# A margin between an operand's planned time and TensorE's step, and durations taken from the trace, in the planner of an encoder block

## The chip, the cores and the metric

The kernel runs on one core of a Trainium2 chip. The metric is the device time of one launch in microseconds (us). Before the change three runs gave 1043.59, 1044.0 and 1044.48 us; the median is 1044.0. The execution that was profiled took 1043.74 us; its span, which the profile's times count from, is 1042.0 us.

## The reference

One layer of an encoder over 528 rows (16 meta tokens and 512 tokens) of 1024 channels, in float32. Two attention branches read the same normalized input and one projection matrix; gates merge them; a mixture of 16 experts follows, in which each expert picks 66 of the 528 rows.

```python
u = rms_norm(h, g_mix)
qa, ka, va, qb, kb, vb, ga, gb = split(u @ w_in)
# branch a: 8 differential heads, d = 64, values of 128
p = softmax(q k^T / 8 - slope * distance)      # two maps per head
oa = rms_norm((p[0] - lam * p[1]) @ va, g_subln) * (1 - lam_init)
# branch b: 8 query heads over 2 key/value heads, d = 128
qh = axial_rope(rms_norm(qb, g_qnorm)); kh = axial_rope(rms_norm(kb, g_knorm))
ob = softmax(qh kh^T / sqrt(128)) @ vb
h = h + (sigmoid(ga) * (oa @ w_branch_a) + sigmoid(gb) * (ob @ w_branch_b)) @ w_out
h = h + expert_choice_ffn(rms_norm(h, g_ffn), w_router, w_gate, w_up, w_down)
return rms_norm(h, g_final)[meta rows dropped]
```

## The kernel before

Every float32 operand is split into a high and a low part (`u_h`, `u_l`; `wh`, `wl`), and each product is three matmuls: high by high, low by high, high by low. A projection of 128 channels runs over 8 chunks of the depth and over two halves of the 528 columns (256 and 272), so a half is 24 rows `pz<-u_h,wh`, `pz<-u_l,wh`, `pz<-u_h,wl` on TensorE. In the names, `pz`, `psc` and `ptr` are the PSUM tiles, two buffers of each: `pz` for projections, values and spread norms, `psc` for scores, `ptr` for transposes.

The work goes in this order. The input is normalized and transposed. Then come 8 differential heads: a head's scores (`psc<-kbuf,qh`), its exponentials (`sn`), their transposes (`ptr<-ident,sn`), the value product (`pz<-wth,vh`, ...), and its norm over channels (`pz<-sqh,sel`; the sums turned by `ptr<-ident,rows`; a root by GpSimd's pow on `cols`; `pz<-ident,cols`). Between a head's steps stand the projections of the next head. For a head, copies between partitions on SyncE's queue lay out its queries and keys (`kbuf<-qh`, `kbuf<-ql`, `qh<-ql`, `kbuf<-kbuf`, `kbh<-kbuf`). Then come 8 GQA heads: scores (`psc<-kbh,qh`), exponentials into `pb` by ScalarE, a scaling of `pb` by the reciprocal sums on VectorE, a small copy (`widen`), transposes (`ptr<-ident,pb`), and the value product, mixed with the projections of the next head's queries and with the products of branch a's output (`pz<-oah,wh`, ...). Then the gates, the output product, the router and the experts.

The program text doesn't set the order within an engine. Each instruction is recorded by a planner, the class `Pace`, which keeps a planned time for each engine (`t`) and for each operand (`ready`), with durations estimated by `Op.price` and a fixed latency of 220 ns (`LAT`) between engines. Instructions of TensorE and DMA starts are put out as the program calls them (`Pace.call`); those of ScalarE, VectorE and GpSimd wait in a list and are put out by `Pace.pump` when their planned start comes within 200 ns of TensorE's planned time (`AHEAD`), by a priority. All instructions pass through one line, L199 in the profile, so a line tells nothing and rows are read by tile names.

TensorE's order comes from `mix`. It has the head's own steps (`main`), the other products as filling (`fill`, in pieces of 6 rows) and small tasks (transposes, value products, norms), which `tick` steps whenever `ok` lets them. `ok` is where a step is held back: all its operands must be planned ready (`pace.when`) by TensorE's planned time, and the PSUM buffers it needs must be free. While a step is held, filling goes ahead of it. On the chip each engine takes its own instructions in the order so fixed and waits where an operand isn't there.

```python
def ok(need, own=None):
    now = pace.now()
    if any(pace.when(a) > now for a in need.tiles):
        return False
...
Task(weigh(i, wt, combine, f"av{NH + h - 1}", ...), Need([ls, p]), ["sn"])
```

`spare_engine` chooses GpSimd or VectorE for some products (`wl`) by GpSimd's planned time, so it reads the same estimates.

Of the kernel before, what the change touches and what calls it, by code (L numbers as in the profile page):

```python
# [15 lines left out]
OP = mybir.AluOpType  # L16
# [69 lines left out]
class Op:  # L86
    def __init__(self, eng, op, fn, args, kw, prio):
        self.eng, self.op, self.fn, self.args, self.kw, self.prio = eng, op, fn, args, kw, prio
        aps = [getattr(a, "ap", a) if isinstance(a, bass.IndirectOffsetOnAxis) else a
               for a in list(args) + list(kw.values())]  # L90
        aps = [a for a in aps if isinstance(a, bass.AP)]
        outs = [kw["out"] if "out" in kw else args[0]]
        if kw.get("accum_out") is not None:
            outs.append(kw["accum_out"])
        self.outs = outs
        self.writes = set().union(*map(keys, outs))
        self.names = self.writes.union(*map(keys, aps))
        self.tiles = {a.name for a in aps + outs}
        self.cost = self.price(aps)

    def price(self, aps):
        n = 1
        for d in self.outs[0].shape[1:]:
            n *= d
        if "dma" in self.op:
            return (CAP * D if "indirect" in self.op else n * self.outs[0].shape[0]) * 4 / 360.0
        if self.op == "transpose":
            return aps[1].shape[0] / 1.2
        if self.eng == "tensor":
            n = 1  # L110
            for d in self.kw["rhs"].shape[1:]:
                n *= d
            return max(107.0, n / 2.4 + 2.5)
        if self.eng == "scalar":
            return 65.0 + n / 1.2 + (90.0 if len(self.outs) > 1 else 0.0)
        if self.eng == "gpsimd":
            return 60.0 + n * 2.27
        if self.op in ("tensor_scalar", "tensor_copy", "memset"):
            return 60.0 + n * 0.65
        return 60.0 + max([n] + [a.free_size() for a in aps if callable(a.free_size)]) / 0.96  # L120
# [5 lines left out]
class Pace:  # L126
# [5 lines left out]
    def __init__(self):  # L132
        self.t = {}
        self.ready, self.by, self.used, self.floor, self.slots = {}, {}, {}, {}, {}
        self.pending, self.busy = [], set()
        self.prio = 1

    def now(self):
# [36 lines left out]
    def start(self, op):  # L175
        start = self.t.get(op.eng, 0.0)
        dma = "dma" in op.op
        for a in op.tiles:
            start = max(start, self.floor.get(a, 0.0) + self.LAT)
        for a in op.names:  # L180
            lat = self.LAT if dma or self.by.get(a) != op.eng else 0.0 if op.eng == "tensor" else 130.0
            start = max(start, self.ready.get(a, 0.0) + lat)
        return start

    def emit(self, op):
        start, eng = self.start(op), op.eng
        if "dma" in op.op:
            issue = 500.0 if eng != "gpsimd" else 1000.0 if "indirect" in op.op else 1300.0
            self.t[eng] = max(self.t.get(eng, 0.0), start if eng == "gpsimd" else 0.0) + issue
            lead = issue + 650.0 if eng == "gpsimd" else 1300.0  # L190
            self.t["dma"] = max(self.t.get("dma", 0.0), start + lead) + op.cost
            end, eng = self.t["dma"] + 850.0, "dma"
        else:
            end = self.t[eng] = start + op.cost
        for a in op.tiles:
            self.used[a] = max(self.used.get(a, 0.0), end)
        for a in op.writes:
            self.ready[a], self.by[a] = end, eng
        op.fn(*op.args, **op.kw)  # L199
# [93 lines left out]
def block_kernel(ctx: ExitStack, tc: tile.TileContext, x, meta_tokens, g_mix, w_cols,  # L293
# [3 lines left out]
    pace = Pace()  # L297
# [45 lines left out]

    tasks = []

    def ok(need, own=None):
        now = pace.now()
        if any(pace.when(a) > now for a in need.tiles):
            return False
        if any(n in t.holds for n in need.names for t in tasks if t is not own):  # L350
            return False
        if need.sn and sum("sn" in t.holds for t in tasks) >= need.sn:
            return False
        return all(n == 0 or pace.free(("psum", tag), 2, n) <= now for tag, n in need.res)
# [13 lines left out]
    def tick():  # L368
        for t in list(tasks):
            if t in tasks and ok(t.need, t):  # L370
                t.step()
# [48 lines left out]
    def mm(out, lhsT, rhs, start, stop, **kw):  # L420
        nc.tensor.matmul(out, lhsT=lhsT, rhs=rhs, start=start, stop=stop, **kw)
# [523 lines left out]
    def mix(main, fill, nfill, steps=5):  # L945
        done, i, fneed = 0, 0, None
        need = next(main)
        while main is not None or fill is not None:
            tick()
            if main is not None and (need is None or (fill is None or done >= i * nfill / steps) and ok(need)):  # L950
                i += need is not None
                try:
                    need = next(main)
                except StopIteration:
                    main = None
            elif fill is not None and (fneed is None or ok(fneed) or not wait()):
                try:
                    fneed = next(fill)
                    done += fneed is None
                except StopIteration:  # L960
                    fill = None
            elif fill is not None:
                pass
            elif not wait():
                if tasks:
                    force()
                else:
                    need = None
# [486 lines left out]
    for r in range(rounds):  # L1455
        rsl = slice(8 * r, 8 * r + 8)
        now, nxt = ping[(r + 1) % 2] if r else pf[:2 * NE, :HL], ping[r % 2]
# [279 lines left out]
    a, b = slice(0, 768), slice(768, D)  # L1737
# [51 lines left out]
```

## Time and profile before

| | before |
|---|---|
| median of three runs | 1044.0 us |
| profiled execution, span | 1043.74 us, 1042.0 us |
| TensorE busy in the span | 958.8 us (92%) |
| TensorE busy, 28 to 571 us | 512.63 of 543.00 us |
| VectorE, ScalarE, GpSimd busy, 28 to 571 us | 355.02, 307.57, 188.75 us |

The profile is one execution. PE is TensorE, DVE VectorE, ACT ScalarE, POOL GpSimd, SP SyncE. A row of the timeline has a start, a length and an operation; in brackets stand the idle time of its engine just before it and what ended that. PEclk is the share of full speed that TensorE's clock was granted. A matmul's length is longer than the distance to the next one, since matmuls overlap; what a row costs is read from the distance of two starts. The stretch from 28 to 571 us holds the two attention branches with their projections, up to the last GQA head.

### The profile page before, as it was taken

What the parts mean: (1) busy time and instruction counts of PE and PEld (TensorE: products, weight loads), DVE (VectorE), ACT (ScalarE), POOL (GpSimd) and SP (SyncE); (2) the same over time, 40 slices, a digit from 0 to 9 for tenths busy, and PEclk for the clock granted to TensorE, in tenths of its full rate; (3) what the DMA queues carried; (4) which work ended last, traced back from release to release, by engine and by line L of the source; (5) the groups of instructions that cost most, each with busy time, mean ns of one, the idle gap of its engine ahead of it and who ended that gap; (6) DMA issues with size and microseconds to landing.
All of it is one profiled execution on the core that took longest, in us unless ns stands there. A gap on an engine that the chain in (4) does not pass through costs nothing.

```text
span 1042.0 us, 18075 instructions
## 1 busy us (share of the span) xinstructions
PE 958.8 (92%) x6835; PEld 830.5 (80%) x6835; DVE 729.0 (70%) x1390; ACT 629.6 (60%) x1297; POOL 311.3 (30%) x354
## 2 busy tenths in 40 slices
PE   4799999999999999999999999995699999999994
PEld 4799989999988899999999999994356666666563
DVE  6357777767774766665665336557699999999886
ACT  5366656666665545555545533344488888888784
POOL 3233232322443434423332400000324342423141
PEclk9999999999999999999999999998799999999997
DMA  7543544444122122121122464834799999999965
GB/s 253 161 136 94 144 124 121 123 108 125 57 72 72 52 72 71 52 72 52 62 62 63 139 201 165 321 121 165 237 355 372 354 374 353 371 348 364 369 218 182
DMA packets 59617, 186.43 MB, mean 179 GB/s; under 512 B 6766, under 2 KB 6907, under 8 KB 59530
## 3 DMA queue, kind: packets, MB, share of 16 engines
q0 software_dynamic: 26544, 98.37, 27.3%
q1 hardware_dynamic: 32378, 84.74, 26.2%
q10 hardware_dynamic: 608, 2.16, 0.7%
q8 instruction: 54, 0.88, 0.3%
q14 instruction: 33, 0.27, 0.1%
HBM read 164.23 MB, written 10.76 MB: 168 GB/s over the span
## 4 chain that ended last, share of the span: by engine, by line
PE 65%; DVE 15%; ACT 7%; issue 4%; POOL 4%; DMA 3%; SPq 1%; POOLq 0%; ACTq 0%; DVEq 0%
PE pz L199 40%; PE psc L199 21%; PE ptr L199 5%; DVE sn L199 3%; POOL cols L199 3%; ACT sn L199 2%; DVE cols L199 1%; DVE pb L199 1%; SPq L199 1%; DVE wtl L199 1%; DVE ls L199 1%; DVE zb L199 1%; DMA zp<-zb 1%; DMA xin<-in_x_dram 1%; POOL wl L199 1%
## 5 line engine op out<-in xcount | busy, mean ns | idle before, releaser
L199 PE MATMUL pz<-u_h,wh 128*128 128x256 f32 (+1 forms) x832 | 246.2, 296 | 5.9 <-ACT u_h L199 1.8
L199 POOL TENSOR_TENSOR wl<-wraw,wh 128x512 fp32r<-128x512 f32 x106 | 142.1, 1347 | 345.9 <-ACT wh L199 341.0
L199 PE MATMUL pz<-u_l,wh 128*128 128x256 f32 (+1 forms) x832 | 238.1, 286 | 0.5 <-DVE u_l L199 0.5
L199 PE MATMUL pz<-u_h,wl 128*128 128x256 f32 (+1 forms) x832 | 238.0, 286 | 0.6 <-DVE wl L199 0.6
L199 DVE TENSOR_TENSOR el<-raw,eh 128x1024 fp32r<-128x1024 f32 x180 | 212.8, 1224 | 8.1 <-ACT eh L199 7.2
L199 ACT CAST eh<-raw 128x1024 fp32r<-128x1024 f32 x180 | 181.3, 1049 | 20.6 <-PE pz L199 13.5
L199 PEld LDWEIGHTS pz<-u_h,wh 128*128 128x128 f32 x832 | 158.1, 190 | 9.2 <-DVE kbuf L199 2.3
L199 PEld LDWEIGHTS pz<-u_l,wh 128*128 128x128 f32 x832 | 158.3, 190 | 0.7 <-DVE u_l L199 0.7
L199 PEld LDWEIGHTS pz<-u_h,wl 128*128 128x128 f32 x832 | 158.1, 190 | 0.8 <-DVE wl L199 0.8
L199 PE MATMUL psc<-eh,xh 128*66 128x512 f32 (+1 forms) x272 | 104.8, 385 | 2.7 <-ACT hid L199 2.2
L199 ACT CAST wh<-wraw 128x512 fp32r<-128x512 f32 x152 | 90.9, 616 | 23.4 <-PE pz L199 19.5
L199 PE MATMUL psc<-el,xh 128*66 128x512 f32 (+1 forms) x272 | 103.8, 381 | 0.1
L199 PE MATMUL psc<-eh,xl 128*66 128x512 f32 (+1 forms) x272 | 103.7, 381 | 0.0
L199 DVE TENSOR_TENSOR wtl<-ptr,wth 128x512 fp32r<-128x512 f32 (+1 forms) x72 | 46.0, 638 | 59.0 <-ACT wth L199 58.7
L199 PE MATMUL pz<-eh,hhl 128*66 128x512 f32 x224 | 70.7, 396 | 0.7 <-DVE hhl L199 0.6
L199 ACT ACTIVATE sn<-sn,nm 128x528 f32<-128x528 f32 x64 | 47.1, 735 | 35.2 <-DVE nm L199 34.8
L199 POOL DMA_INDIRECT acc<-ys,idxu x15 | 27.5, 1835 | 122.0 <-ACT ys L199 97.1
L199 ACT CAST wth<-ptr 128x512 fp32r<-128x512 f32 (+1 forms) x72 | 39.0, 542 | 40.4 <-PE ptr L199 40.0
L199 PEld LDWEIGHTS psc<-eh,xh 128*66 128x66 f32 x272 | 37.4, 137 | 25.1 <-ACT hid L199 3.2
L199 PEld LDWEIGHTS psc<-el,xh 128*66 128x66 f32 x272 | 37.3, 137 | 23.4 <-DVE el L199 0.5
L199 PEld LDWEIGHTS psc<-eh,xl 128*66 128x66 f32 x272 | 37.4, 137 | 21.8 <-DVE xl L199 0.5
L199 DVE CUSTOM_DVE_ANT_0 sn<-psc,m 128x528 f32<-128x528 f32 x64 | 44.1, 695 | 5.8 <-PE psc L199 5.8
(315 smaller groups left out, 2328.3 us busy)
## 6 DMA issues: line engine op xcount, KB each, us to landing
wraw<-in_w_in_dram SPq DMA_DIRECT2D x76, 512.0 KB, 3.6
raw<-in_w_up_dram POOLq DMA_DIRECT2D x14, 2048.0 KB, 17.3
raw<-in_w_down_dram POOLq DMA_DIRECT2D x14, 2048.0 KB, 20.2
raw<-in_w_gate_dram POOLq DMA_DIRECT2D x13, 2048.0 KB, 18.7
m<-in_c_bias_dram SPq DMA_DIRECT2D x8, 1056.0 KB, 7.0
kbuf<-kbuf SPq DMA_DIRECT2D x32, 132.0 KB, 2.4
raw<-in_w_up_dram SPq DMA_DIRECT2D x2, 2048.0 KB
raw<-in_w_gate_dram SPq DMA_DIRECT2D x2, 2048.0 KB, 10.5
```

The source lines that it names most:

```text
L199: op.fn(*op.args, **op.kw)
```

## The change

`ok` adds a margin, SLACK = 600 ns: an operand must be planned ready that long before TensorE's planned time. The estimates in `Op.price` take other durations: a matmul 0.4375 ns a column plus 6 (at least 109) instead of 1/2.4 plus 2.5 (at least 107), ScalarE 75 ns more for an activation and 30 for a copy, GpSimd 1150 ns for a pow and 30 ns more for the rest. And a VectorE operation with at least two operands, all in SBUF, that would start within GpSimd's latest operation is planned at that operation's end (`port`). No operation is added to the computation; the list of instructions comes out in another order.

```diff
--- before.py
+++ after.py
@@ -97,6 +97,8 @@
         self.names = self.writes.union(*map(keys, aps))
         self.tiles = {a.name for a in aps + outs}
         self.cost = self.price(aps)
+        ins = [a for a in aps if not a.name.startswith(("pz", "psc", "ptr"))]
+        self.port = eng == "vector" and "dma" not in op and len(ins) >= 2 and len(ins) == len(aps)
 
     def price(self, aps):
         n = 1
@@ -110,11 +112,14 @@
             n = 1
             for d in self.kw["rhs"].shape[1:]:
                 n *= d
-            return max(107.0, n / 2.4 + 2.5)
+            return max(109.0, n * 0.4375 + 6.0)
         if self.eng == "scalar":
-            return 65.0 + n / 1.2 + (90.0 if len(self.outs) > 1 else 0.0)
+            scaled = 75.0 if self.op == "activation" else 30.0
+            return 65.0 + scaled + n / 1.2 + (90.0 if len(self.outs) > 1 else 0.0)
         if self.eng == "gpsimd":
-            return 60.0 + n * 2.27
+            if self.kw.get("op") == OP.pow:
+                return 1150.0
+            return 90.0 + n * 2.27
         if self.op in ("tensor_scalar", "tensor_copy", "memset"):
             return 60.0 + n * 0.65
         return 60.0 + max([n] + [a.free_size() for a in aps if callable(a.free_size)]) / 0.96
@@ -133,6 +138,7 @@
         self.t = {}
         self.ready, self.by, self.used, self.floor, self.slots = {}, {}, {}, {}, {}
         self.pending, self.busy = [], set()
+        self.pool = 0.0, 0.0
         self.prio = 1
 
     def now(self):
@@ -180,6 +186,8 @@
         for a in op.names:
             lat = self.LAT if dma or self.by.get(a) != op.eng else 0.0 if op.eng == "tensor" else 130.0
             start = max(start, self.ready.get(a, 0.0) + lat)
+        if op.port and self.pool[0] < start < self.pool[1]:
+            start = self.pool[1]
         return start
 
     def emit(self, op):
@@ -192,6 +200,8 @@
             end, eng = self.t["dma"] + 850.0, "dma"
         else:
             end = self.t[eng] = start + op.cost
+            if eng == "gpsimd":
+                self.pool = start, end
         for a in op.tiles:
             self.used[a] = max(self.used.get(a, 0.0), end)
         for a in op.writes:
@@ -343,9 +353,11 @@
 
     tasks = []
 
+    SLACK = 600.0
+
     def ok(need, own=None):
         now = pace.now()
-        if any(pace.when(a) > now for a in need.tiles):
+        if any(pace.when(a) + SLACK > now for a in need.tiles):
             return False
         if any(n in t.holds for n in need.names for t in tasks if t is not own):
             return False
```

Below, rows of each engine's order before and of the changed kernel; the line is L199 before and L209 in the changed kernel.

SyncE's queue at the start, before: `wraw` are loads of projection weights, `m` of the position bias, the rest are the first head's copies between partitions.

```order
L199 DMA wraw<-in_w_in_dram 128x1024 x3
L199 DMA kbuf<-qh 64x528
L199 DMA kbuf<-ql 64x528
L199 DMA qh<-ql 64x528
L199 DMA kbuf<-kbuf 64x528 x2
L199 DMA kbh_204<-kbuf 64x528 x2
L199 DMA wraw<-in_w_in_dram 128x1024
L199 DMA kbuf<-kbuf 64x528 x2
L199 DMA m_197<-in_c_bias_dram 128x4x528
```

The changed kernel, the same place:

```order
L209 DMA wraw<-in_w_in_dram 128x1024 x2
L209 DMA kbuf<-qh 64x528
L209 DMA kbuf<-ql 64x528
L209 DMA wraw<-in_w_in_dram 128x1024
L209 DMA qh<-ql 64x528
L209 DMA kbuf<-kbuf 64x528 x2
L209 DMA kbh_204<-kbuf 64x528 x2
L209 DMA kbuf<-kbuf 64x528 x2
L209 DMA wraw<-in_w_in_dram 128x1024
L209 DMA m_197<-in_c_bias_dram 128x4x528
```

The first two copies moved ahead of one load of weights, and the last two ahead of another.

TensorE in the GQA head around 414 us, at the second score product of the head; `pz<-oah,wh` and the rows like it are the products of branch a. Before:

```order
L199 MATMUL psc<-kbh_202,qh 128x264
L199 MATMUL psc<-kbl_203,qh 128x264
L199 MATMUL psc<-kbh_202,ql 128x264
L199 MATMUL ptr<-ident,pb 128x128 x4
L199 MATMUL ptr<-ident,pb 48x128
L199 MATMUL pz<-oah,wh 128x272
L199 MATMUL pz<-oal,wh 128x272
L199 MATMUL pz<-oah,wl 128x272
```

The changed kernel, the same head (eight rows of the branch product of 272 columns stand where the mark is):

```order
L209 MATMUL psc<-kbh_202,qh 128x264
L209 MATMUL psc<-kbl_203,qh 128x264
L209 MATMUL psc<-kbh_202,ql 128x264
L209 MATMUL pz<-oah,wh 128x272
L209 MATMUL pz<-oal,wh 128x272
L209 MATMUL pz<-oah,wl 128x272
...
L209 MATMUL pz<-oah,wl 128x272
L209 MATMUL ptr<-ident,pb 128x128 x4
L209 MATMUL ptr<-ident,pb 48x128
```

The transposes of `pb`, which followed the score product directly, now follow 12 rows of the branch product.

VectorE in the next GQA head, from where the norm's sums arrive (`cols_8x<-ptr`) to the scaling of `pb`; `cols<-cols_8x` takes up GpSimd's root. Before:

```order
L199 TENSOR_SCALAR cols_80<-ptr 128x4
L199 TENSOR_SCALAR cols_80<-ptr 16x1
L199 TENSOR_TENSOR ql<-zb,qh 128x528
L199 TENSOR_SCALAR cols<-cols_80 128x5 x2
L199 RECIPROCAL ls<-ls 128x1
L199 TENSOR_SCALAR pb<-pb,ls 128x528
L199 SCALAR_TENSOR_TENSOR m_197<-m_197,pz 128x256
L199 TENSOR_REDUCE nmb<-psc 128x1
```

The changed kernel:

```order
L209 RECIPROCAL ls<-ls 128x1
L209 TENSOR_SCALAR pb<-pb,ls 128x528
L209 TENSOR_SCALAR cols_81<-ptr 128x4
L209 TENSOR_SCALAR cols_81<-ptr 16x1
L209 SCALAR_TENSOR_TENSOR m_197<-m_197,pz 128x256
L209 TENSOR_REDUCE nmb<-psc 128x1
L209 TENSOR_TENSOR wtl<-ptr,wth 128x4x128
L209 SCALAR_TENSOR_TENSOR wm<-ptr,sign,stk 48x128
L209 TENSOR_TENSOR nmb<-nmb,cols 128x1
L209 TENSOR_SCALAR cols<-cols_81 128x5 x2
```

The scaling of `pb` came behind the root's result and now stands ahead of the sums' arrival; the root's result is taken up after it and after a further reduction and a pair of transposes' evictions.

## Rows read from the trace of the kernel before

**Rows 1.** Busy time and share of the span, from the page's first part
```profile
PE 958.8 (92%) x6835; PEld 830.5 (80%) x6835; DVE 729.0 (70%) x1390; ACT 629.6 (60%) x1297; POOL 311.3 (30%) x354
```

**Rows 2.** Windows: length; busy us (instructions) of PE, PEld, DVE, ACT, POOL; clock; DMA; GB/s
```profile
28.00:571.00 543.00, 512.63 (x4153) 499.90 (x4152) 355.02 (x812) 307.57 (x816) 188.75 (x216) 0.99 0.32 90
...
281.00:385.00 104.00, 97.03 (x777) 93.33 (x777) 68.23 (x145) 57.41 (x149) 46.96 (x59) 1.00 0.22 63
```

**Rows 3.** Waits of TensorE in 28 to 571 us: total, times, longest
```profile
PE ptr L199 <- DVE pb L199: 8.2, 7, 1.4
PE pz L199 <- POOL cols L199: 8.0, 8, 1.4
PE psc L199 <- DMA kbuf<-kbuf: 6.2, 1, 6.2
PE pz L199 <- DVE kbuf L199: 1.7, 3, 0.7
```

**Rows 4.** Timeline of TensorE at the start: start, length, operation, [idle before <- releaser]
```profile
40.03 0.28 PE L199 MATMUL pz<-u_h,wh 128*128 128x256 f32 x1
40.15 0.28 PE L199 MATMUL pz<-u_l,wh 128*128 128x256 f32 x1
...
49.12 1.47 PE L199 MATMUL psc<-kbuf,qh 128*128 128x264 f32 x4 [6.25 <-DMA kbuf<-kbuf]
...
51.27 0.41 PE L199 MATMUL pz<-u_h,wh 128*128 128x256 f32 x1
51.48 0.41 PE L199 MATMUL pz<-u_l,wh 128*128 128x256 f32 x1
```

**Rows 5.** Windows around the first score product
```profile
48.00:50.00 2.00, 0.88 (x3) 0.72 (x4) 0.00 (x0) 0.00 (x0) 0.00 (x0) 0.50 1.06 305
...
54.00:56.00 2.00, 2.00 (x17) 2.00 (x17) 1.15 (x3) 0.60 (x2) 0.00 (x0) 0.91 0.00 0
```

**Rows 6.** Timeline of SyncE's queue at the start
```profile
34.25 0.33 SPq L199 DMA_DIRECT2D wraw<-in_w_in_dram  x1
34.63 0.56 SPq L199 DMA_DIRECT2D kbuf<-qh  x1
...
39.67 0.46 SPq L199 DMA_DIRECT2D qh<-ql  x1
...
56.98 0.47 SPq L199 DMA_DIRECT2D kbuf<-qh  x1
...
59.26 0.46 SPq L199 DMA_DIRECT2D qh<-ql  x1
```

**Rows 7.** Timeline of VectorE at the start
```profile
31.77 0.44 DVE L199 TENSOR_TENSOR ql<-pz,qh 128x272 fp32r<-128x272 f32 x1 [1.14 <-ACT qh L199]
32.87 1.30 DVE L199 TENSOR_TENSOR wl<-wraw,wh 128x512 fp32r<-128x512 f32 x1 [0.65 <-ACT wh L199]
```

**Rows 8.** Timeline of several engines in a steady GQA head
```profile
408.00 0.49 PE L199 MATMUL ptr<-ident,rows 128*128 128x128 f32 x3
...
409.04 1.17 POOL L199 TENSOR_TENSOR cols<-cols,halfs 128x5 f32<-128x5 f32 x1 [1.95 <-DVE cols L199]
...
411.27 2.52 POOL L199 TENSOR_TENSOR wl<-wraw,wh 128x512 fp32r<-128x512 f32 x2
...
411.34 1.32 DVE L199 TENSOR_SCALAR cols<-cols 128x5 f32<-128x5 f32 x2 [1.17 <-POOL cols L199]
...
412.76 1.32 DVE L199 TENSOR_SCALAR pb<-pb,ls 128x528 f32<-128x528 f32 x1
...
414.23 0.73 PE L199 MATMUL ptr<-ident,pb 128*128 128x128 f32 x5 [1.42 <-DVE pb L199]
...
416.74 0.50 DVE L199 TENSOR_SCALAR pb<-pb,ls 128x528 f32<-128x528 f32 x1
```

**Rows 9.** Timeline of TensorE in the second and third differential head
```profile
136.29 0.76 PE L199 MATMUL pz<-ident,cols 128*128 128x128 f32 x5 [1.15 <-POOL cols L199]
...
152.65 0.39 PE L199 MATMUL pz<-u_h,wh 128*128 128x272 f32 x1 [0.81 <-ACT oa L199]
```

## The prediction

> **What bounds the kernel now.** I read the page first: TensorE is busy for 958.8 us, 92% of the span [rows 1]. A reorder can therefore only take TensorE's idle time, and only where the order of its rows differs. In the order of the changed kernel TensorE's rows are those of before from about 579 us on, so the second look was at the stretch before that: from 28 to 571 us TensorE is busy for 512.63 of 543.00 us, idle for 30.4 [rows 2]. That is the room, and 104 us of it (281 to 385) hold 7.0 [rows 2]. Third, the waits of that stretch [rows 3]: 8.2 us for pb (the exp'd scores of a GQA head after DVE has scaled them), 8.0 for cols (POOL's root of the norm), 6.2 in one piece for the first head's kbuf copies, and 1.7 for kbuf; the table's last groups (oa, sql, zv and other small ones) 4.5 us. All are waits of TensorE for an operand made by another engine, or for a PSUM slot that such an engine clears. So the reader is to see that TensorE is the bound, with holes, and that each hole names its maker.
>
> **The change part by part.** It adds and removes no instruction of any weight; it moves them. Where the margin asks that an operand be ready 600 ns before TensorE's planned time, the planner puts other rows (projection or branch products) ahead of the step that waits. A row of 256 columns costs 0.12 us at full clock [rows 4], so 6 rows put 0.7 us and 12 rows 1.4 to 1.5 us in front.
>
> *The start.* TensorE waits 6.25 us until 49.12 for the first score product, for DMA kbuf<-kbuf [rows 4]. The granted clock in 48 to 50 us is 0.50, the lower of the two levels (1.2 GHz), after TensorE had stood still, and in 54 to 56 it is 0.91 [rows 5]. 0.09 short of 1 over 2 us is 0.36 us at half, so the low stretch lasts from 49.12 to 54.36, 5.2 us, and half of that, 2.6 us, is lost; the rows show it, 0.21 us apart against 0.12 [rows 4]. Both hang on SyncE's queue. There the first copy, kbuf<-qh, goes out at 34.63, behind a weight load that left at 34.25 [rows 6]. That load waited for its buffer: DVE's wl product began at 32.87 and took 1.30, until 34.17 [rows 7]. But the copy's data were done at 31.77 + 0.44 = 32.21 [rows 7]. In the changed order the two copies stand ahead of that load, so they can go at 32.2, 2.4 us earlier. The next step, qh<-ql, went at 39.67, 5.0 us after the first copy; in the second head it goes 2.3 us after (56.98 to 59.26), with no load on the queue just ahead of them [rows 6]. With 2.3 the step goes at 34.6 in place of 39.67, 5.1 us earlier, and everything behind it too: the score product could start at 44.0. With 5.0 it goes at 37.2 and the product at 46.7. TensorE comes to it at 49.12 - 6.25 = 42.87, plus six projection rows that now stand ahead: 43.6. So the wait is 0.4 us (then no drop of the clock) or 3.1. I take the first, since the second head's rows are the same copies without a load ahead: 6.25 - 0.4 + 2.6 = **8.4 us** off. Bounds: 8.9 (nothing left) and 3.1 (wait of 3.1, clock still falling).
>
> The Trainium skill ("DMA: Bandwidth & Descriptors", section on queues, rings and completion order) says that descriptors on one ring of an SDMA engine are consumed in ring order. The 5.0 against 2.3 us agree with it: the small copy stood behind 512 KB. It also speaks against me, since that load now stands ahead of qh<-ql and the copies after it: by it the product would start up to 2.7 us later (5.0 less 2.3), the term would be 5.7 and the time 1027.0 instead of 1024.3.
>
> *The GQA heads.* Five heads wait 1.41 us or so each at the same step: the rows' transposes at 408.00, POOL's pow 409.04 (1.17 us) and four small POOL operations, DVE's scaled cols at 411.34 (1.32 us), the scaling of pb at 412.76 (1.32 us, beside two POOL products of 2.52 us together from 411.27; 0.50 at 416.74, after them), TensorE at 414.23 after a wait of 1.42 [rows 8]. In the changed order DVE scales pb before it takes POOL's root (cols) in all these heads, so the wait for POOL (1.17 us) and the 1.32 us of cols are off pb's path. In two of them 12 branch rows besides stand between the score product and the transposes of pb, 1.5 us more cover against 1.42 of wait; there a wl product (1.30 us, as at 32.87 [rows 7]) has come ahead of the scaling on DVE. So I count the whole group, **8.2 us** [rows 3]. If pb is late again in half of the seven, it is 4.
>
> A rule that speaks against this term: the Trainium skill ("SBUF — State Buffer", section SBUF: two separate sides) has the port pair that VectorE shares with GpSimd as an exclusive lock for the whole instruction. The two lengths of the scaling, 1.32 and 0.50 us, agree in kind: DVE takes longer while POOL multiplies. The planner's new port test only delays a DVE operation that starts inside POOL's latest operation. What the rule makes of the time is the third rival.
>
> *The waits for cols.* Eight, together 8.0 us [rows 3]: four in the differential heads, all like that of 1.15 us at 136.29 [rows 9], so 4.6, and 3.4 in the turn from one branch to the other. In the changed order the first head has 42 rows in place of 34 between the transposes of rows and the product on cols (-1.1). In the others there are 22 for 34 and 29 for 42, some 1.5 us less cover; but a POOL product (1.26 us, half of the 2.52 [rows 8]) that stood between pow and the small operations now stands ahead of pow. The two cancel, and I count nothing there; of the turn's 3.4 us I count half, since most of its distances grow: **2.8 us**. Bounds: a loss of 4 (five heads that had no such wait get 0.8) and a gain of 6.
>
> *The other waits.* Kbuf's three waits and the small ones (oa, sql, zv and so on) add to 6.2 us [rows 3]; half lie in the turn, where the margin moves rows ahead. I take **2 us**; bounds 0 and 4.
>
> *What the order adds.* The value product of 272 columns now comes 6 rows behind that of 256 in most differential heads (12 before, in some). Six rows are 0.7 us, and the wait for oa was 0.81 us where ACT came to it late [rows 9]. I count **2 us** of new waits over all 16 heads; bounds 0 and 8 (ten such waits). The margin puts no wait on an engine's queue: it is only read while the order is made. The new prices of ACT and POOL alone move operations between DVE and POOL (a wl product goes to DVE in some heads, 1.3 us as at 32.87 [rows 7]); DVE is busy for 355.02 of the 543 us [rows 2], so I give that no price of its own; where it stands ahead of pb it is in the bound of that term.
>
> The sum: -8.4 - 8.2 - 2.8 - 2 + 2 = **-19.4 us**. Against the profiled execution's 1043.74 us (span 1042.0) that is 1024.3; the median of the runs, 1044.0, is 0.3 above it. I predict 1024.5.
>
> **The rivals.**
> 1. *Only the start comes free.* The planner's times are sums of estimates; with higher prices its clock for TensorE moves too, and the margin may be eaten by errors that add up over a head. For it: the scaling of pb took 1.32 us at one place and 0.50 at another [rows 8]. Against: the moves stand at the very place of the wait. Then -8.4, and 1 us of new waits: 1036.3.
> 2. *Slots take the place of operands.* With rows of projections pulled forward, the two PSUM buffers of a kind are asked for sooner after their last use. For it: 0.81 us for oa, a wait for a slot [rows 9]. Against: in the waits of before, pb, cols and the copies make 22.4 of the 28.6 us [rows 3]. At 0.8 us in each of 16 heads it adds 12.8 rather than 2 to the sum: -8.6, 1035.
> 3. *The shared port.* If POOL's product again falls on the scaling of pb in the five heads, 0.82 us each (1.32 less 0.50) stay, 4.1 us: 1028.4.
> 4. *Slower: the filling runs out.* A head has a fixed number of foreign rows to be mixed in. What the margin puts early is missing at the head's end, where the chain from rows to pb (408.00 to 414.23, 6.2 us [rows 8]) or the value product then has nothing beside it. It decides from the point where this uncovered piece is over 1.2 us a head in 16 heads, 19.4 us. At 1.42, the longest wait of this kind now, it is 22.7: 1047. Against it: in the changed order the branch rows still reach each head's end.
> 5. *It does nothing.* The margin would have to leave the order alone; the rows of the changed kernel show that it doesn't, so this has a chance only as gains and losses that cancel.
>
> **How the numbers follow.** The forecast 0.56 (its own range 1019 to 1030); the first rival 0.10 and the second 0.12; the third 0.14; the fourth 0.04; the fifth 0.04. The low end is every term at its better bound: -8.9 - 8.2 - 6 - 4 = -27.1, so 1016.6; the high end takes in rivals 1 to 3 (1036.3). I set 1016.5 to 1036.5. What a measurement of this kernel can tell from no change is about 0.2%, 2 us: faster by more than that 0.92, within it 0.04, slower 0.04.
>
> **What would show it.** In the profile after: the first score product at 43.5 to 45 us with a wait under 1 us, and no slice of PEclk at 0.5 behind it; if the wait is over 3 us, the start's term is wrong. In the table of waits, pb under 2 us in all and no 1.4 us wait repeated in the GQA heads; cols at about 5 us, still in the differential heads; TensorE idle for about 13 to 15 us between 28 us and the end of the last GQA head, which comes near 552. New waits for oa, zv or kbuf over 6 us in all would speak for the second rival; DVE's scaling of pb at 1.3 us again, with pb in the waits, for the third. Any difference after the gates (the order there is unchanged) would contradict the whole reading.

## The result, and the profile after

The changed kernel took 1035.01 us (median of four, 1032.82 to 1037.56), before 1044.24: a ratio of 0.9913, with a 95% interval of 0.9886 to 0.994. That is 9.2 us faster, where 19.5 were forecast: inside the range, but less than half the size. Its profiled execution took 1036.38 us, span 1034.6. One of the six executions of e14, further down, took 1582.62 us at a granted clock of 0.56; it is in that run's median (1037.92) and not in its ratio, and the other five have a median of 1036.55.

By the page's first part TensorE is busy for 960.1 us, 93% of the span. In the stretch that was the room for the change (columns as in [rows 2]):

```profile
28.00:571.00 543.00, 520.98 (x4232) 508.87 (x4232) 335.90 (x815) 308.02 (x823) 191.69 (x217) 1.00 0.33 92
```

22.0 us idle, where there were 30.4 [rows 2]: 8.4 us went. The table of waits in the same stretch (total, times, longest) says which:

```profile
PE ptr L209 <- DVE wtl L209: 5.9, 6, 2.2
PE pz L209 <- POOL cols L209: 3.2, 6, 1.1
PE psc L209 <- DMA kbuf<-kbuf: 2.8, 2, 1.5
PE pz L209 <- DVE kbuf L209: 2.6, 2, 1.3
PE ptr L209 <- ACT sn L209: 2.4, 3, 0.8
PE pz L209 <- DVE zb L209: 1.9, 2, 1.6
PE pz L209 <- DVE oa L209: 1.6, 2, 1.4
```

Pb is gone from it (8.2 us [rows 3]), cols fell from 8.0 to 3.2, the copies from 6.2 to 2.8. But 5.9 us for wtl are new, 2.4 for sn, 1.9 for zb, and kbuf rose from 1.7 to 2.6. Wtl is VectorE's part of emptying a transpose's PSUM tile, so transposes now wait for a buffer where they waited for their operand. (The table takes in waits over 0.15 us. VectorE's oa, 1.6, is new as well; ScalarE's oa, sqb and zv have 1.1 left.)

**The start.** TensorE's two waits (start, length, operation, idle before and its releaser), against one of 6.25 us [rows 4]:

```profile
44.03 0.36 PE L209 MATMUL psc<-kbuf,qh 128*128 128x264 f32 x1 [1.52 <-DMA kbuf<-kbuf]
45.66 1.03 PE L209 MATMUL psc<-kbuf,qh 128*128 128x264 f32 x3 [1.27 <-DMA kbuf<-kbuf]
```

SyncE's queue, against [rows 6]:

```profile
30.68 0.56 SPq L209 DMA_DIRECT2D kbuf<-qh  x1
...
33.16 0.34 SPq L209 DMA_DIRECT2D wraw<-in_w_in_dram  x1
33.55 0.46 SPq L209 DMA_DIRECT2D qh<-ql  x1
...
35.40 1.20 SPq L209 DMA_DIRECT2D kbh<-kbuf  x2
39.73 1.28 SPq L209 DMA_DIRECT2D kbuf<-kbuf  x2
41.11 0.57 SPq L209 DMA_DIRECT2D wraw<-in_w_in_dram  x1
41.73 0.46 SPq L209 DMA_DIRECT2D m<-in_c_bias_dram  x1
```

The first copy goes at 30.68 and qh<-ql 2.87 us later, where 2.3 were forecast. But the copies into kbh, issued at 35.40, stand behind the load of 33.16, and the last pair goes only at 39.73, 4.3 us after them (1.9 before: 43.45 after 41.51). Then a load and the bias go out right behind that pair, and it lands 4.6 us after the second one's issue. The clock, against [rows 5]:

```profile
44.00:46.00 2.00, 0.70 (x2) 0.53 (x3) 0.00 (x0) 0.00 (x0) 0.00 (x0) 0.89 1.01 284
46.00:48.00 2.00, 2.00 (x10) 2.00 (x10) 1.11 (x3) 0.52 (x1) 0.00 (x0) 0.50 1.03 394
48.00:50.00 2.00, 2.00 (x15) 2.00 (x14) 1.64 (x6) 1.14 (x4) 0.00 (x0) 0.75 0.42 151
```

0.11 short of 1 in the first window is 0.44 us at half, then 2.0, then 0.25 short, 1.0 us: 3.4 us low, 1.7 lost, instead of 5.2 and 2.6.

**The GQA heads.** Rows of three engines around the longest new wait, in the order of their starts (zb and zp are parts of a later head's queries, which VectorE and GpSimd turn by the position's angle; qh is made from them):

```profile
487.76 0.71 DVE L209 TENSOR_TENSOR zb<-zb,zp 128x528 f32<-128x528 f32 x1 [1.22 <-POOL zp L209]
...
488.50 0.63 ACT L209 CAST qh<-zb 128x528 fp32r<-128x528 f32 x1 [3.61 <-DVE zb L209]
...
489.04 0.58 ACT L209 CAST wth<-ptr 128x512 fp32r<-128x512 f32 x1
...
489.65 0.69 DVE L209 TENSOR_TENSOR wtl<-ptr,wth 128x512 fp32r<-128x512 f32 x1 [1.18 <-ACT wth L209]
...
490.39 0.55 PE L209 MATMUL ptr<-ident,rows 128*128 128x128 f32 x3 [2.21 <-DVE wtl L209]
```

The transposes of rows need the PSUM buffer that the first four transposes of pb at 485.23 filled. To empty it ScalarE casts wth first (489.04) and VectorE then takes the rest (489.65). But ScalarE's queue has the cast of qh ahead of it, and that waits until zb is done (488.47), 3.61 us idle. The buffer is late because of an instruction of another chain, queued ahead of the one that frees it. In e1, the same order, ScalarE idles 2.14 us at this place and TensorE 0.75.

**The differential heads.** The scaling of sn twice, GpSimd's product beside the second, and what follows:

```profile
144.62 0.77 DVE L209 SCALAR_TENSOR_TENSOR sn<-sn,ls 128x528 f32<-128x528 f32 x1
...
145.72 1.28 POOL L209 TENSOR_TENSOR wl<-wraw,wh 128x512 fp32r<-128x512 f32 x1 [8.83 <-ACT wh L209]
...
145.75 1.81 DVE L209 SCALAR_TENSOR_TENSOR sn<-sn,ls 128x528 f32<-128x528 f32 x1
...
147.60 0.22 ACT L209 COPY sn<-sn 128x32 f32<-128x32 f32 x1 [1.05 <-DVE sn L209]
...
148.04 0.35 ACT L209 CAST kbuf<-pz 128x256 fp32r<-128x256 f32 x1
...
148.90 0.39 PE L209 MATMUL pz<-wth,vh 128*128 128x272 f32 x1 [1.28 <-DVE kbuf L209]
```

VectorE's scaling takes 0.77 us alone and 1.81 beside GpSimd's product, which began 0.03 us earlier. ScalarE's copy behind it comes 1.05 us late, the kbuf cast behind that too, and the value product waits 1.28 us for its PSUM buffer. Two heads do this (148.90 and 214.74). The kernel before has scalings as long, up to 1.91 us, and no wait over 0.71 us for kbuf: what is new is what stands behind them. Two more of the new waits have a lengthened VectorE operation beside a GpSimd product on their chain: ls, 1.34 us at 298.90 where others take 0.22, ahead of the 1.40 us for oa (301.75), and kbl, 1.57 us at 356.13 where another takes 0.69, ahead of the 1.65 us for zb (357.84).

### The profile page after: what moved, and what is told of

Same layout as the page of the kernel before. It is cut to its first block, busy times and chain, and to the rows that moved or that the text cites. A ratio compares the mean times of both kernels' runs of the same rounds, so it can differ in the third digit from the quotient of the medians.

```text
span 1034.6 us, 18078 instructions
## 1 busy us (share of the span) xinstructions
PE 960.1 (93%) x6835; PEld 831.6 (80%) x6835; DVE 710.8 (69%) x1393; ACT 627.4 (61%) x1297; POOL 312.5 (30%) x351
## 5 line engine op out<-in xcount | busy, mean ns | idle before, releaser
L209 PE MATMUL pz<-u_h,wh 128*128 128x256 f32 (+1 forms) x832 | 245.8, 295 | 5.2 <-DVE zb L209 1.6
L209 PE MATMUL pz<-u_h,wl 128*128 128x256 f32 (+1 forms) x832 | 237.7, 286 | 1.1 <-POOL wl L209 1.1
L209 PE MATMUL pz<-u_l,wh 128*128 128x256 f32 (+1 forms) x832 | 237.7, 286 | 0.3 <-DVE u_l L209 0.3
L209 POOL TENSOR_TENSOR wl<-wraw,wh 128x512 fp32r<-128x512 f32 x103 | 139.3, 1362 | 306.6 <-ACT wh L209 298.2
L209 DVE TENSOR_TENSOR el<-raw,eh 128x1024 fp32r<-128x1024 f32 x180 | 211.6, 1216 | 17.3 <-ACT eh L209 17.0
L209 ACT CAST eh<-raw 128x1024 fp32r<-128x1024 f32 x180 | 181.4, 1048 | 22.2 <-PE pz L209 10.9
L209 PEld LDWEIGHTS pz<-u_h,wh 128*128 128x128 f32 x832 | 157.8, 190 | 8.4 <-DVE zb L209 1.9
L209 PEld LDWEIGHTS pz<-u_h,wl 128*128 128x128 f32 x832 | 157.6, 189 | 1.3 <-POOL wl L209 1.3
L209 PEld LDWEIGHTS pz<-u_l,wh 128*128 128x128 f32 x832 | 158.0, 190 | 0.6 <-DVE u_l L209 0.6
L209 PE MATMUL psc<-eh,xh 128*66 128x512 f32 (+1 forms) x272 | 105.8, 389 | 3.9 <-ACT hid L209 3.4
L209 PE MATMUL psc<-eh,xl 128*66 128x512 f32 (+1 forms) x272 | 104.9, 386 | 0.0
L209 PE MATMUL psc<-el,xh 128*66 128x512 f32 (+1 forms) x272 | 104.7, 385 | 0.0
L209 ACT CAST wh<-wraw 128x512 fp32r<-128x512 f32 x152 | 90.6, 616 | 21.4 <-PE pz L209 18.0
L209 DVE TENSOR_TENSOR wtl<-ptr,wth 128x512 fp32r<-128x512 f32 (+1 forms) x72 | 45.9, 638 | 64.8 <-ACT wth L209 64.5
L209 ACT ACTIVATE sn<-sn,nm 128x528 f32<-128x528 f32 x64 | 47.0, 735 | 44.5 <-DVE nm L209 43.9
L209 PE MATMUL pz<-eh,hhl 128*66 128x512 f32 x224 | 71.0, 396 | 2.3 <-ACT hhl L209 1.7
L209 POOL DMA_INDIRECT acc<-ys,idxu x15 | 25.8, 1717 | 125.5 <-ACT ys L209 60.0
L209 PEld LDWEIGHTS psc<-eh,xh 128*66 128x66 f32 x272 | 38.1, 140 | 26.5 <-ACT hid L209 4.3
L209 PEld LDWEIGHTS psc<-el,xh 128*66 128x66 f32 x272 | 37.9, 139 | 23.2 <-issue 0.6
L209 PEld LDWEIGHTS psc<-eh,xl 128*66 128x66 f32 x272 | 38.0, 140 | 21.8 <-issue 0.6
L209 DVE TENSOR_TENSOR wl<-wraw,wh 128x512 fp32r<-128x512 f32 x49 | 36.1, 738 | 25.1 <-ACT wh L209 14.3
L209 ACT CAST wth<-ptr 128x512 fp32r<-128x512 f32 (+1 forms) x72 | 38.8, 539 | 16.4 <-PE ptr L209 15.7
## 6 DMA issues: line engine op xcount, KB each, us to landing
raw<-in_w_gate_dram SPq DMA_DIRECT2D x2, 2048.0 KB, 10.5
```

## The experiments

Medians of the runs; before 1044.1 to 1044.7 in each call. The ratio is that of the run to before.

| run | median us | ratio, 95% interval |
|---|---|---|
| e1 the changed kernel again | 1033.07 | 0.9885 (0.987 to 0.9901) |
| e2 margin only | 1044.98 | 1.0007 (0.9997 to 1.0018) |
| e3 durations and port rule only | 1040.12 | 0.9957 (0.9942 to 0.9973) |
| e4 load behind the copies | 1031.42 | 0.988 (0.9857 to 0.9904) |
| e5 experts' stage with durations of before | 1031.74 | 0.9872 (0.9858 to 0.9887) |
| e6 before, experts' stage with the new | 1043.61 | 0.9994 (0.9981 to 1.0007) |
| e7 margin on buffers too | 1038.46 | 0.9946 (0.9928 to 0.9965) |
| e8 e4 and e5 together | 1030.57 | 0.9861 (0.9846 to 0.9875) |
| e9 margin and pow's duration | 1033.75 | 0.9892 (0.9878 to 0.9906) |
| e10 e8, margin on buffers in the GQA heads | 1024.7 | 0.9806 (0.9792 to 0.982) |
| e11 e10, margin 1000 in the differential heads | 1039.71 | 0.9952 (0.9937 to 0.9967) |
| e12 without the port rule | 1044.83 | 0.9999 (0.9988 to 1.001) |
| e13 margin 500 | 1032.5 | 0.9887 (0.9865 to 0.991) |
| e14 margin 700 | 1037.92 | 0.9933 (0.9912 to 0.9954) |
| e15 e10 without the port rule | 1031.33 | 0.9879 (0.9861 to 0.9898) |

**e1.** No edit. 

> The changed kernel as it is, profiled and timed once more. TensorE reached the experts' first transposes 10.6 us earlier than before, but the span was only 7.4 us shorter: the experts' stage took some 4 us longer although its order is the same. Theory A: that stage hangs on the rate of the weight loads, which differs between executions; then another profile shows another length of it (281 to 287 us from the transposes of xs to the last products), and the times spread over several us, 1032 to 1038. Theory B: the new order lengthens the stage itself, for instance by where its first loads start; then it is about 286 us again, and the time within 1 us of 1035.

1031.08 to 1038.66: the spread of theory A. But the stage's length repeats, as theory B has it: from the transposes of xs to the end the profiled execution took 306.5 us, the first one 306.2, and before 303.0. Another part of the spread is TensorE's clock. The windows of e1 at the third differential head, whose wait for kbuf ends at 150.55:

```profile
150.00:152.00 2.00, 1.45 (x8) 1.45 (x9) 0.42 (x1) 0.04 (x1) 0.63 (x1) 0.74 0.33 47
152.00:154.00 2.00, 2.00 (x10) 2.00 (x10) 0.00 (x0) 0.40 (x2) 0.00 (x0) 0.50 0.55 215
154.00:156.00 2.00, 2.00 (x16) 2.00 (x16) 0.71 (x1) 1.06 (x2) 0.00 (x0) 0.90 0.00 0
```

The waits are those of the first profile (0.29 and 1.28 us), where the clock stayed up. Here it fell behind them: 0.26 short of 1 is 1.04 us at half, then 2.0, then 0.4, so 3.4 us low and 1.7 lost. The trace of the kernel before has no such fall in its differential heads.

**e2, e3, e9.** e2 is `before` with the new line in `ok`; e3 has `SLACK = 0.0`; e9 is e2 with

```diff
         if self.eng == "gpsimd":
-            return 60.0 + n * 2.27
+            return 1150.0 if self.kw.get("op") == OP.pow else 60.0 + n * 2.27
```

> Only the margin of 600 ns; durations as before, no port rule. Theory A: the margin is what moves the steps behind more rows, so most of the gain is here, 6 to 11 us below before, with pb's waits of 1.4 us gone; the start's copies leave early as well, but the last two stand behind a weight load, so the first score product still waits 3 us or more. Theory B: the margin needs the traced durations to be right (pow 1.15 us planned as 0.07), so alone it gives little, under 4 us, and the 1.4 us waits stay.

> Only the durations and the port rule; margin 0. The copies at the start stand behind the third weight load as before. Theory A: the start's 6 us wait and the clock's fall stay, and the gain is under 5 us, from the GQA heads' pb (the root is now planned at its length, so pb is scaled ahead of it). Theory B: most of the gain, 7 us or more, is in the durations.

> The margin, and of the new durations only that of GpSimd's pow (1150 ns, was about 71). Theory A: the margin alone gained nothing because the root was planned 1.1 us too short: its product on cols stood 5 rows behind the transposes of rows and waited 2.5 us in three heads, with the clock falling behind it. With pow priced right these waits go and the time comes to 1035 to 1039. Theory B: the other durations and the port rule matter as much; then it stays above 1040.

The margin alone gains nothing: theory B on the time, though pb's 1.4 us waits, which it let stay, are gone. In three heads the product on cols stands directly behind the transposes of rows and zv and waits 2.5 us, as here, with the clock falling behind it (1.12 us for its four rows):

```profile
100.86 1.12 PE L199 MATMUL pz<-ident,cols 128*128 128x128 f32 x4 [2.57 <-POOL cols L199]
```

e3 has a gain of 4.3 us (theory A), with 3.7 us of waits for the copies left of the 6.2 that it let stay. Two things in its trace, which has no margin, bear on the changed kernel. The waits for wtl are there already, four of the six ahead of the transposes of rows in the GQA heads (431.07 to 520.40):

```profile
PE ptr L209 <- DVE wtl L209: 6.5, 6, 1.8
```

And pb's waits are gone, though four of the five scalings that TensorE waited 1.4 us for still come behind the root's result, as here, at 0.49 us in place of 1.32 and with 24 branch rows ahead of the transposes:

```profile
464.98 0.24 DVE L209 TENSOR_SCALAR cols<-cols 128x5 f32<-128x5 f32 x2 [0.85 <-POOL cols L209]
...
465.64 0.49 DVE L209 TENSOR_SCALAR pb<-pb,ls 128x528 f32<-128x528 f32 x1
...
466.87 0.71 PE L209 MATMUL ptr<-ident,pb 128*128 128x128 f32 x5
```

With the length of pow alone e9 reaches 1033.75, under theory A's range and as good as the changed kernel; its waits for cols are 3.7 us where e2 has 10.5. So beside the margin the root's length is enough here, without the other durations. It is not enough in every order: e12 has it too and gains nothing.

**e4.** The sixth weight load is kept back until the first head's last copy into kbuf has been put out:

```diff
+        if kind == "wraw" and self.loads == 6:
+            self.held = op
+            self.pending.append(op)
+            return
...
+        if kind == "kbuf" and self.copies == 6 and self.held in self.pending:
+            self.pull(self.held)
```

> The changed kernel with one move: the weight load that still stood ahead of the first head's copies within the key tile goes behind the last of them; TensorE's order is the same. Theory A: the small copies were held by the 512 KB ahead of them on the queue; then the last pair starts at about 37.5 instead of 39.7 us, the first score product waits under 0.5 us, the clock stays up, and it is 3 to 4.5 us faster than the changed kernel up to the router. Theory B: the copies take their 4 us each for another reason (traffic of other loads, their own 64 rows); then the wait stays at 2 us or more and the gain is under 1 us, or the load comes late for its product and the wait moves there.

SyncE's queue, and the clock where it had fallen:

```profile
33.42 0.46 SPq L210 DMA_DIRECT2D qh<-ql  x1
...
35.33 1.18 SPq L210 DMA_DIRECT2D kbh<-kbuf  x2
37.01 1.83 SPq L210 DMA_DIRECT2D kbuf<-kbuf  x2
38.92 1.03 SPq L210 DMA_DIRECT2D wraw<-in_w_in_dram  x2
```

```profile
44.00:46.00 2.00, 2.00 (x18) 2.00 (x17) 2.00 (x6) 1.09 (x3) 0.00 (x0) 1.00 1.01 395
46.00:48.00 2.00, 2.00 (x18) 2.00 (x17) 1.26 (x4) 0.87 (x4) 0.00 (x0) 1.00 1.03 339
```

The last pair goes at 37.01, 1.7 us after the copies into kbh, TensorE waits 0.35 us in all, the clock stays at 1.00. Theory A holds for the start: the first head's transposes of rows come at 90.83 for 94.57. Up to the router only part of it was left in this execution, since the clock fell later, at 210 and at 488 us, behind waits of 1.28 and 2.33; and the median is 1.6 us below e1's, less than the spread of either.

**e5, e6, e8.** A switch sets the durations and the port rule back from the experts' gather on (e5), sets them in only there (e6), or does e4 and e5 (e8).

> The changed kernel up to the gather of the first expert's rows; from there on the durations of before, which gives VectorE and ScalarE the order that they had before in the experts' stage (their last 500 and 398 instructions; TensorE, GpSimd and SyncE have one order in all these kernels there). Theory A: the stage is longer because of the loads' rate alone, so it stays at 304 to 307 us from the transposes of xs to the end and the time is that of the changed kernel, 1032 to 1035 with a spread of several us. Theory B: the traced durations reorder the casts there and cost 3 to 4 us; then the stage is 303 us again as before, the time 1030 to 1031.5, and the spread 1 to 2 us.

> The reverse: the kernel before up to the experts, the changed kernel's order of VectorE and ScalarE in their stage. Theory A: no difference from before, 1043 to 1045. Theory B: 3 to 4 us slower than before, 1046 to 1048, and a wider spread.

> The weight load behind the first head's copies, and the experts' stage with the durations of before: the two repairs together. Theory A of the first (the load held the copies, worth 1 to 2 us: the first score product was 1.3 us earlier than in the changed kernel's trace and 3 earlier than in its second one) and theory B of the second add up: 1028 to 1030. If the experts' stage hangs on the loads alone, what is gained ahead of it is lost there, 1031 to 1034.

The transposes of xs begin the stage. In the changed kernel (span 1034.6), in e5 (span 1030.3) and in e6 (span 1046.2):

```profile
728.43 1.11 PE L209 MATMUL ptr<-ident,xs 66*128 66x66 f32 x8 [7.16 <-DMA xs<-urow,idxu]
```

```profile
727.43 1.11 PE L212 MATMUL ptr<-ident,xs 66*128 66x66 f32 x8 [7.41 <-DMA xs<-urow,idxu]
```

```profile
739.79 1.11 PE L212 MATMUL ptr<-ident,xs 66*128 66x66 f32 x8 [7.42 <-DMA xs<-urow,idxu]
```

From there to the end it is 306.2, 302.9 and 306.4 us. Over all profiles the old order of casts gave 302.8 to 303.8 (eight executions), the new one 301.4 to 307.1 (nine; in e12 two of VectorE's instructions are exchanged). So it widens the spread, and costs some 3 us in four of nine; in e6's median it costs nothing (1043.61, spread 1040.96 to 1049.19). Theory B is right on the spread and wrong on the median; why one order gives two lengths stays open. e8 is where both repairs were said to add up, 1028 to 1030: 1030.57, just above.

**e7.** `pace.free(("psum", tag), 2, n) + SLACK <= now` in `ok`. 

> The changed kernel with the margin of 600 ns also on PSUM buffers coming free. Theory A: the waits that replaced those of before are for buffers (transposes behind VectorE's wtl, 5.9 us; kbuf, zb, oa and sn some 8): with the margin on them too, wtl falls under 2 us and the time up to the router is 4 to 6 us shorter. Theory B: they come from the chain itself being late, and a margin on buffers only moves them on to other operands; then the idle time of TensorE in 28 to 571 us stays at 20 us or more.

```profile
PE pz L209 <- POOL cols L209: 4.3, 2, 2.1
PE ptr L209 <- DVE ls L209: 2.5, 2, 1.2
...
PE ptr L209 <- DVE vl L209: 2.1, 2, 1.1
```

No wait over 0.15 us is left between 368 and 582 us, so in the GQA heads theory A holds. In the differential heads it makes waits of 2.1 us for cols and others, with four falls of the clock: neither theory foresaw that, and the gain is smaller than the changed kernel's. (28 to 571 us hold 18.4 us of idle time, where theory B had 20 or more.)

**e10, e11.** `slot[0]` takes SLACK's place in that line and is 0 until the GQA heads begin, then 600; e11 has 1000 for the margin before that. 

> The load behind the copies, the old durations in the experts' stage, and the margin on PSUM buffers in the GQA heads only. Theory A: there it removed all of TensorE's waits between 368 and 582 us, while in the differential heads it made waits of 2.1 us; so here 3 to 4.5 us below e8, 1026 to 1028. Theory B: what the buffers' margin wins in the heads it loses in the turn before them (it had a wait of 0.7 and one of 0.6 us there); then 1029 to 1032.

> As e10, with a margin of 1000 ns in the differential heads and 600 in the GQA heads. Theory A: the waits left in the differential heads (0.79 for sn, 1.28 for kbuf, 1.15 for cols) are longer than the margin covers, since VectorE's and ScalarE's queues run later than planned; with 400 ns more about half of their 8 us goes, 2 to 4 us below e10. Theory B: they come from what stands ahead on those queues, not from the size of the margin; the order changes and the waits come at other places with the same sum, within 2 us of e10, either way.

Waits in e10, and its stretch:

```profile
PE pz L213 <- POOL cols L213: 2.9, 5, 1.2
PE pz L213 <- DVE kbuf L213: 2.6, 2, 1.3
PE ptr L213 <- ACT sn L213: 2.4, 3, 0.8
PE ptr L213 <- DVE wtl L213: 1.5, 2, 0.9
```

```profile
28.00:571.00 543.00, 527.84 (x4299) 517.41 (x4299) 341.58 (x832) 315.19 (x838) 190.87 (x217) 1.00 0.33 94
```

15.2 us idle. At 1024.7 it is the fastest, 20.0 us below before, under theory A's range. e11 is outside both theories: four waits for cols, 8.2 us in all, 15 us slower than e10.

**e12, e15.** The two lines of the port rule in `start` left out, from the changed kernel and from e10. 

> The changed kernel without the port rule. Theory A: the rule seldom acts, since it looks only at a VectorE operation that would start inside GpSimd's latest one, and VectorE's long operations mostly start first; within 2 us of the changed kernel. Theory B: the rule is what spares the scaling of pb its 0.8 us; without it pb waits come back and it is 3 to 6 us slower, 1036 to 1040.

> The fastest kernel so far (load behind the copies, old durations in the experts' stage, margin on buffers in the GQA heads) without the port rule. Theory A: without the rule the changed kernel lost its gain through waits for transposes' buffers in the GQA heads (7.5 us) and for cols in the differential ones (1.5 us, three times); the buffers' margin takes care of the first kind, so the GQA heads stay free of waits and only the differential heads are worse: 1027 to 1033. Theory B: the rule works on the operands' lengths themselves; then waits for pb or wtl come back in the GQA heads and it is over 1035.

Without the rule the whole gain is gone, which neither theory had. But the waits of e12 are for wtl and cols,

```profile
PE ptr L207 <- DVE wtl L207: 8.5, 7, 3.0
PE pz L207 <- POOL cols L207: 5.1, 4, 1.5
```

not for pb; and in e15 wtl is down to one wait and the time is 13.5 us lower (with e4's and e5's edits in it):

```profile
PE pz L211 <- POOL cols L211: 4.6, 3, 1.5
...
PE ptr L211 <- DVE wtl L211: 0.7, 1, 0.7
```

So the rule doesn't act on the scaling's length (theory A of e15). It tips the order: with margin and pow alone it isn't needed (e9), with the other durations it is (e12), and where buffers are covered it is worth 6.6 us (e15 against e10), all ahead of 362 us.

**e13, e14.** `SLACK = 500.0` and `700.0`. 

> The changed kernel with a margin of 500 ns. Theory A: the size of the gain beyond the start and the pb waits is an accident of the order that comes out, since each step is held or let go in whole pieces of 6 rows; then 100 ns less moves the time by several us either way, 1029 to 1042, with new waits at other places. Theory B: the gain is a smooth function of the margin; then 1032 to 1036.

> The changed kernel with a margin of 700 ns. As before: theory A 1029 to 1042 and not on a line with 500 and 600; theory B 1031 to 1036.

1032.5 and, over e14's other five executions, 1036.55, with 1033 to 1035 between, which is within or just beyond theory B: these two don't decide. E12 against e9 does: 11 us between two orders from lists of prices that differ little.

## Why the prediction was wrong

Whole and parts, in us, measured by the profile:

| step | forecast | measured |
|---|---|---|
| start: wait and clock | -8.4 | -3.5 and -0.9 |
| pb | -8.2 | -8.2 |
| cols | -2.8 | -4.8 |
| the other waits | -2 | in the next line |
| what the order adds | +2 | +3.4 for kbuf, sn, zb, oa and the small ones net, and +5.9 for wtl |
| sum | -19.4 | -8.1 |

TensorE came to the first transposes of xrow, among the gates' rows, 10.2 us earlier (579.56 for 589.73). Of the 2.1 us beyond the table's sum, 1.1 were there before the two orders part (their last common row starts at 40.25 for 41.34), and 0.8 is a wait for pb at 571.22 in the kernel before, just behind the table's stretch. Behind the gates 3.2 us were lost again in this execution (306.2 for 303.0 in the experts' stage). The median gained 9.2 and 11.4 us in the two sets. Of the 11.3 us between -19.4 and -8.1, the start makes 4.0 and the last two terms 9.3; cols gave 2.0 more than counted.

- *What bounds the kernel, and where the room is* was right: the gain lies ahead of 572 us, and it is made of the waits named. That nothing could differ after the gates was wrong: only TensorE's order is the same there (from 606.42 us on, 616.71 before, and not from 579: the transposes of xrow stand elsewhere among the gates' rows), and VectorE's and ScalarE's casts changed by the new durations (e5, e6).
- *The start* was mis-sized, -8.4 for -4.4. The step that failed is "with 2.3 the step goes at 34.6, and everything behind it too": the first copies and qh<-ql were early, but the load then stood ahead of the next ones. The sentence beside it on the ring order of the Trainium skill ("DMA: Bandwidth & Descriptors", section Queues, rings and completion order) gave 5.7, and the trace agrees with it in kind: the copies issued 2.24 us behind the load let their successor go only after 4.3 us. I had weighed it and left it out of the sum. e4 removes exactly this, and the start then has the size that was forecast.
- *The GQA heads*: pb's 8.2 us went as forecast, but that the scaling ahead of cols is what does it is not shown. "In all these heads" was a misreading: in the first of the five it still comes behind the root's result (402.82 after 401.60) and isn't waited for, and in e3 that is so in four of the five. There the scaling takes 0.49 to 0.50 us in place of 1.32, and more rows stand ahead of the transposes; how much each does stays open.
- *What the order adds* is the step that failed. "I count 2 us of new waits": it was 14.4 by the table, 12.0 for PSUM buffers (wtl 5.9, kbuf ahead of the value product 2.6, zb 1.9, VectorE's oa 1.6) and 2.4 for an operand (sn). Against them the small waits of before gave back 5.1, where 2 were counted. That is the second rival, slots in place of operands, at close to its 12.8 us; that it also meets its 1035 is luck, since the start fell short by 4.0 and cols and the small waits gave 5.1 more. I gave it 0.12 because the waits of before were for operands. But the margin is only on operands: the buffer that a transpose will write is asked for without one. e7 and e10 show that this is what can be mended: with the margin on buffers the GQA heads lose every wait, and the time comes to 1024.7. That the margin brought these waits about is not shown: of wtl, the largest, the durations alone have 6.5 us (e3) and the margin alone 3.4 (e2), where the kernel before has none. Which of the two does it in the changed kernel stays open.
- *The shared port* (third rival) is there, at another place: sn in the differential heads, 1.81 us for 0.77. The Trainium skill's exclusive lock ("SBUF — State Buffer", section SBUF: two separate sides) agrees with it in kind: the scaling took 1.04 us more beside a product of 1.28; kept out until the product's end, it would have taken 1.25 more. The planner's rule misses it, since it sees only an operation planned to start inside GpSimd's. This was read from rows and not tried. At pb the scaling is still 1.3 to 1.6 us long at places, and nothing waits there.
- *Slower, the filling runs out*: not seen.

## What to carry over

Covering one kind of condition leaves the waits to the kinds that aren't covered: transposes waited 0 us for wtl before, 3.4 with the margin on operands alone (e2) and 6.5 with the new durations alone (e3). Before adding a margin, list everything that a step needs (operands, buffers, what is queued ahead on the engine that frees them) and put it on all of them, stage by stage. Price the longest single link of the chain first; here one duration (pow) stood between a margin that gained 11 us and one that gained nothing (e9, e2). When one list of prices orders a whole program, look at every engine's order in every stage, also where the bounding engine's is unchanged; and take a result of a few us from one order as one draw, since e9 and e12 are 11 us apart.

## What the hardware showed

TensorE's clock fell to 0.50 behind a wait as short as 1.28 us (with one of 0.29 us shortly ahead) in e1, and did not in another execution of the same kernel with the same waits; that fall cost 1.7 us. In the first head a 132 KB copy within SBUF took 1.7 us (e4, 35.33 to 37.01) to 2.9 (the changed kernel, 30.68 to 33.55) to be followed by its successor when no load stood just ahead of it on the queue, and 4.3 to 5.0 behind a 512 KB load. VectorE's scaling of sn, 0.77 us alone, took 1.81 beside a GpSimd product of 1.28.
